# A transformer layer whose feed-forward products are taken seven at a time: the order of the seven, their PSUM banks, one held weight tile, and where W2's left factors are summed

## The chip, the cores and the metric

One core of a Trainium2 chip runs the whole layer in one program. The number given for a kernel is the device time of one execution, in microseconds (us).

## The reference, cut to what matters

The layer has 512 tokens of width 2048 and a feed-forward width of 8192, all in float32:

```python
mix = concat(rms_norm(windowed attention), rms_norm(dilated attention)) @ w_o
h   = layer_norm(ALPHA * x + mix)
ff  = square(relu(h @ w1)) @ w2                     # 2048 -> 8192 -> 2048
ple = (p @ w_ple) * sigmoid(h @ w_ple_gate)         # gate: 2048 -> 2048
out = layer_norm(ALPHA * h + ff + ple)
```

Only the gate, W1, W2 and the last norm are touched by the change. The attention part, up to 736.8 us, is the same text in both kernels.

## The kernel before, in words

**Seven products.** The gate, W1 and W2 are cut into 18 calls of `strassen`: two for the gate, eight for W1 (one for each chunk `n` of 1024 hidden columns), eight for W2 (`m` = 0 to 3 picks two chunks as the inner dimension, `c` = 0 or 1 the half of the output columns; the order is m0c0, m0c1, m1c0 and so on). A call multiplies a left matrix (tokens x inner) by a block of weights by Winograd's form of Strassen's method: each side is cut in four quarters, sums of quarters are the seven left factors s1 to s7 and the seven right factors, and the seven products p1 to p7 are added up into four quarters of the output. A product is summed over four slices `k` of the inner dimension, so a call has 28 steps (p, k) of 12 matmuls each: float32 is split into a high and a low part on either side, and three of the four part products are taken (`L598`, `L600`, `L601`).

**Right factors.** For each `k` the quarters b11, b12 and b22 are loaded (`wr` by SP's queue, `wk` by POOL's), and DVE makes b12 - b11 (`L610`) and b22 minus that (`L611`, kept in `wk`). In the second phase b21, b12 and b22 are loaded, b12 for the second time and b22 too, and DVE makes b22 - b12 (`L618`) and b21 - `wk` (`L619`). Every right factor is split by ACT (`wh`, `L579`) and DVE (`wl`, `L580`), with three buffers of each. `wr` has seven buffers and `wk` four.

**Left factors.** `factors` loads quarter blocks (`qh` of h for the gate and W1, `qf` of the squared hidden for W2, by ACT's queue at `L671`), forms s5, s6, s7 and s3 by DVE sums (`L547` to `L566`) and splits each factor by ACT (`L534`) and DVE (`L535`). For W2 this is done once for each `m`, with fourteen block loads and ten sums: the first half (s1, s5, s6) in the c = 1 call of the `m` before, the second half (s2, s7, s3, s4) in the first steps of the c = 0 call that uses them.

**PSUM and what reads it.** Three tiles a, b and c take the products: c holds p1 and then p2 on top of it, a holds p6, p7, p4 summed, b holds p5 and p3. In the gate and W1, `quarters` copies or adds what is complete into SBUF. In the gate the finished quarter is combined with `ple` and with `hk`, a block of h that TensorE transposes (`L693`). In W1 a finished quarter is transposed (`L707`), relu'd by ACT and squared by DVE (`L709`), and stored to `f_d`. In W2, ACT copies each product out (`ev`, `L793`) and POOL's queue adds it into DRAM (`z_d`, and `p1_d` for p1). For the last `m`, `last_sum` adds in SBUF instead: it loads `zl` from `z_d`, adds the products (`L740`), takes the norm's statistics, and `finish` writes two of the four token rows at a time.

**What sets the order.** `PHASES` fixes the order of the 28 steps; dictionaries of `between` steps (`mid`, `last`) hang the left factors' work in front of a step's number. All blocks that are not weights (`qh`, `qf`, `hk`, `pl`, the quarters `c`, `f`, `ev`, `zl`) share one pool of six 512 KB buffers, tag "o". A load that finds no free buffer waits on its queue, and what stands behind it in that queue waits with it.

Of the kernel before, what the change touches and what calls it, by code (L numbers as in the profile page):

```python
# [11 lines left out]
F32 = mybir.dt.float32  # L12
# [26 lines left out]
def block_kernel(ctx: ExitStack, tc: tile.TileContext, xT, pT, positions, w_in, w_o, w_gate, w_ple,  # L39
# [448 lines left out]
    for g in range(4):  # L488
        raw = raw_load(w_ple[g])
        wk = [split(raw[:, k * S:(k + 1) * S], "w", "w") for k in range(2)]  # L490
        for t in range(NQ):
# [6 lines left out]
            nc.scalar.dma_start(ple_d[t, g], e)  # L498
# [20 lines left out]
    opc = tc.tile_pool(name="op", bufs=1)  # L519
    op = opc.__enter__()  # L520
    ps = ctx.enter_context(tc.tile_pool(name="ps2", bufs=1, space=bass.MemoryType.PSUM))

    def o_tile(name, shape=(P, 2, S)):
        return op.tile(list(shape), F32, name=name, tag="o", bufs=OB)

    def factors(load, sg):


        q = {}

        def put(p, src):
            hi = sp.tile([P, 4, HS], R32, name=f"s{p}h", tag=f"s{p}h", bufs=2)
            lo = sp.tile([P, 4, HS], R32, name=f"s{p}l", tag=f"s{p}l", bufs=2)
            nc.scalar.activation(hi, src, AF.Copy)  # L534
            nc.vector.tensor_tensor(lo, src, hi.bitcast(F32), op=ALU.subtract)  # L535
            sg[p] = hi, lo

        def get(*ks):
            for k in ks:
                q[k] = load(k)  # L540

        def a1():
# [40 lines left out]
    def strassen(src, sg, read, between={}):  # L583


        bank = {c: ps.tile([P, 2, S], F32, name=c, tag=c, bufs=1) for c in "cab"}
        t2 = {}

        def prod(p, chain, k, w, first):
# [318 lines left out]
```

## Time and profile before

| what | value |
|---|---|
| median of 3 runs | 2374.33 us (2371.89 to 2377.45) |
| the profiled execution | 2366.62 us |
| its span, first to last instruction | 2364.8 us |
| mean granted TensorE clock over the span | 0.965 |
| busy, share of the span: TensorE, DVE, ACT, POOL | 92%, 71%, 43%, 5% |
| attention, up to the first `strassen` call | 736.8 us |
| gate, two calls | 209.4 us |
| W1, eight calls | 663.7 us |
| W2, eight calls | 729.2 us |
| after the last matmul | 25.6 us |

The stages begin and end where the matmuls of the 18 calls begin in the trace. Shares over the whole span hide that the stages differ: the stretches in the rows below, one for each call, are the unit to read. The granted clock is the throttle's: 1.00 is 2.4 GHz, and 0.5 of it is 1.2 GHz.

### The profile page before, as it was taken

The page shows a single profiled execution, that of the slowest core. Times are in us where ns is not written, and L with a number is a line of the kernel's source. Part 1 is how long each engine was busy: PE and PEld are TensorE (multiplying, and loading weights), DVE is VectorE, ACT ScalarE, POOL GpSimd, SP SyncE. Part 2 cuts the span into 40 slices and gives each one's busy share as a digit, 9 for nine tenths or more (in the row PEclk, how much of TensorE's full clock was granted, in tenths as well). Part 3 has the DMA queues.
Part 4 walks back from the last instruction along what each step waited for, and adds up shares of the span by engine and source line. Part 5 has one row for each costly group of instructions (what it writes and reads, how often), then busy time and mean ns, then how long its engine had stood idle before and what let it go on. Part 6 is the DMA issues. An engine that isn't in the chain of part 4 may idle for free. (4 is left out here: it accounts for less than half of the span.)

```text
span 2364.8 us, 26043 instructions
## 1 busy us (share of the span) xinstructions
PE 2171.0 (92%) x9672; PEld 1771.6 (75%) x9672; DVE 1683.8 (71%) x2035; ACT 1015.2 (43%) x1320; POOL 116.7 (5%) x152
## 2 busy tenths in 40 slices
PE   8999999999994988999999999997988988988895
PEld 7888888888873766887888888785766766766674
DVE  7676655555766866777777777779668568667888
ACT  5454443443335433444444444445445445444331
POOL 0000000000020000000000000000101101101000
PEclk9999999999997988999999999998999999988998
DMA  6222222233328656556555545556867867877682
GB/s 224 72 70 74 72 81 81 80 112 134 98 94 315 202 192 225 170 172 206 165 173 186 197 159 179 195 181 234 217 216 229 216 204 237 218 207 233 204 279 77
DMA packets 134943, 406.84 MB, mean 172 GB/s; under 512 B 13184, under 2 KB 24448, under 8 KB 134816
## 3 DMA queue, kind: packets, MB, share of 16 engines
q1 hardware_dynamic: 84512, 270.83, 34.2%
q0 software_dynamic: 22944, 64.08, 11.0%
q10 hardware_dynamic: 27360, 70.26, 8.2%
q8 instruction: 76, 1.25, 0.2%
q14 instruction: 51, 0.42, 0.1%
HBM read 347.45 MB, written 57.67 MB: 171 GB/s over the span
## 5 line engine op out<-in xcount | busy, mean ns | idle before, releaser
L579 ACT ACTIVATE wh<-wr 128x1024 fp32r<-128x1024 f32 x360 | 380.8, 1061 | 553.6 <-PE a L600 232.5
L580 DVE TENSOR_TENSOR wl<-wr,wh 128x1024 fp32r<-128x1024 f32 x360 | 434.9, 1220 | 50.3 <-ACT wh L579 49.6
L65 DVE TENSOR_TENSOR wl<-raw,wh 128x512 fp32r<-128x512 f32 x216 | 149.1, 691 | 163.9 <-ACT wh L64 131.5
L64 ACT ACTIVATE wh<-raw 128x512 fp32r<-128x512 f32 x216 | 135.7, 629 | 283.6 <-PE u L72 271.3
L71 PE MATMUL u<-xh,wh 128*128 128x512 f32 x576 | 227.4, 395 | 6.0 <-ACT xh L64 6.0
L72 PE MATMUL u<-xl,wh 128*128 128x512 f32 x576 | 225.4, 391 | 0.0
L73 PE MATMUL u<-xh,wl 128*128 128x512 f32 x576 | 225.3, 391 | 0.0
L579 ACT ACTIVATE wh<-wk 128x1024 fp32r<-128x1024 f32 x144 | 152.4, 1060 | 167.2 <-PE a L600 73.6
L580 DVE TENSOR_TENSOR wl<-wk,wh 128x1024 fp32r<-128x1024 f32 x144 | 174.6, 1218 | 19.3 <-ACT wh L579 19.3
L618 DVE TENSOR_TENSOR wr<-wr 128x1024 f32<-128x1024 f32 x72 | 88.1, 1223 | 116.2 <-DMA wr<-in_w 108.8
L598 PE MATMUL c<-wh,s1h 128*128 128x512 f32 x288 | 116.7, 405 | 34.3 <-DVE s5l L535 24.9
L610 DVE TENSOR_TENSOR wr<-wr 128x1024 f32<-128x1024 f32 x72 | 87.8, 1222 | 77.9 <-DMA wr<-in_w 73.3
L601 PE MATMUL b<-wl,s3h 128*128 128x512 f32 x288 | 116.2, 403 | 19.2 <-DVE wl L580 19.2
L601 PE MATMUL c<-wl,s1h 128*128 128x512 f32 x288 | 116.5, 404 | 17.7 <-DVE wl L580 17.7
L71 PEld LDWEIGHTS u<-xh,wh 128*128 128x128 f32 x576 | 108.6, 189 | 27.2 <-ACT xh L64 6.0
L611 DVE TENSOR_TENSOR wk<-wk,wr 128x1024 f32<-128x1024 f32 x72 | 87.9, 1220 | 56.6 <-DMA wk<-in_w 45.0
L601 PE MATMUL b<-wl,s5h 128*128 128x512 f32 x288 | 115.0, 399 | 14.0 <-DVE wl L580 14.0
L73 PEld LDWEIGHTS u<-xh,wl 128*128 128x128 f32 x576 | 108.5, 188 | 22.6
L598 PE MATMUL a<-wh,s6h 128*128 128x512 f32 x288 | 114.7, 398 | 11.5 <-ACT wh L579 11.5
L72 PEld LDWEIGHTS u<-xl,wh 128*128 128x128 f32 x576 | 108.6, 189 | 21.9 <-DVE xl L65 0.4
L601 PE MATMUL a<-wl,s6h 128*128 128x512 f32 x288 | 115.4, 401 | 8.9 <-DVE wl L580 8.9
L598 PE MATMUL a<-wh,s7h 128*128 128x512 f32 x288 | 114.0, 396 | 8.7 <-ACT wh L579 8.7
(240 smaller groups left out, 4881.5 us busy)
## 6 DMA issues: line engine op xcount, KB each, us to landing
wr<-in_w SPq DMA_DIRECT2D x320, 512.0 KB, 4.3
raw<-in_w_in SPq DMA_DIRECT2D x64, 512.0 KB, 3.7
wk<-in_w POOLq DMA_DIRECT2D x64, 512.0 KB, 5.0
qf<-f_d ACTq DMA_DIRECT2D x56, 512.0 KB, 5.4
wr<-in_w_gate SPq DMA_DIRECT2D x40, 512.0 KB, 4.7
z_d<-ev POOLq DMA_DIRECT2D x36, 512.0 KB, 8.5
raw<-in_w_o SPq DMA_DIRECT2D x32, 512.0 KB, 3.5
f_d<-f ACTq DMA_DIRECT2D x32, 512.0 KB, 3.5
```

Of the source, the lines that this page charges most:

```text
L64: nc.scalar.activation(hi, src, AF.Copy)
L65: nc.vector.tensor_tensor(lo, src, hi.bitcast(F32), op=ALU.subtract)
L71: nc.tensor.matmul(o, wh, ah, start=start, stop=False)
L72: nc.tensor.matmul(o, wh, al, start=False, stop=False)
L73: nc.tensor.matmul(o, wl, ah, start=False, stop=stop)
L579: nc.scalar.activation(hi, t, AF.Copy)
L580: nc.vector.tensor_tensor(lo, t, hi.bitcast(F32), op=ALU.subtract)
L598: nc.tensor.matmul(o, sh[:, i, x], w[0][:, c], start=first and k == 0 and j == 0, stop=False, skip_group_check=skip)
L601: nc.tensor.matmul(o, sh[:, i, x], w[1][:, c], start=False, stop=k == 3 and j == 1, skip_group_check=skip)
L610: nc.vector.tensor_tensor(t1, t1, b11, op=ALU.subtract)
L611: nc.vector.tensor_tensor(t2[k], t2[k], t1, op=ALU.subtract)
L618: nc.vector.tensor_tensor(t3, b22, t3, op=ALU.subtract)
```

## The change

`PHASES` becomes the flat table `STEPS`, with p3 and p7 in the middle and p2 and p4 last. Tile a now takes p1, p6, p7 and p4 as one running sum, b takes p5 and p3, and c takes p2 alone; a product on a is read between its last step and the next product's first step on a. `READ` says to which quarter each product goes; p1 is added into z's (0, 0) quarter, and `p1_d` is gone.

In W2 (`hold=True`) b12 is loaded once into tag "g" and kept for its second use, so a `k` costs five loads and not six. In W1 and the gate it is loaded twice, through tag "q".

After each W1 chunk the sums of W2's left factors are formed from the four squared quarters, and all seven factors are stored in `s_d` (three stores by ACT's queue, four by POOL's). The square moves from DVE to ACT. W2 then loads fourteen finished factors for each `m` by SP's queue (`qs`, two buffers) and only splits them: twelve in the c = 1 call before, two (`LATE`: s4 and s2 of the second chunk) in the c = 0 call.

The buffers are given out anew: `r` 4 (was `wr` 7), `q` 2, `k` 4, `g` 4, `c` 3, where there were six "o". `z_d` and `ple_d` have two token rows side by side, so that a partition's piece in DRAM is 4 KB and not 2 KB. `last_sum` does seven additions where there were ten, loads `zl` by SP and stores by POOL. `finish` runs for rows 2 and 3 after p4 and for rows 0 and 1 after p2.

```diff
-WB = {"wr": 7, "wk": 4, "wh": 3, "wl": 3}
-OB = 6
+WB = {"r": 4, "q": 2, "k": 4, "wh": 3, "wl": 3, "c": 3, "g": 4}
-    (((1, 0), (1, 1), (5, 0), (6, 0), (1, 2), (5, 1), (6, 1), (1, 3), (5, 2), (6, 2), (6, 3), (5, 3)), 1),
...
+STEPS = ((1, 0), (1, 1), (5, 0), (1, 2), (5, 1), (1, 3), (5, 2), (6, 0), (5, 3), (6, 1), (6, 2), (6, 3),
+         (3, 0), (7, 0), (3, 1), (7, 1), (3, 2), (7, 2), (3, 3), (7, 3),
+         (2, 0), (4, 0), (4, 1), (2, 1), (4, 2), (4, 3), (2, 2), (2, 3))
+LATE = {2: (12, 16), 4: (14, 18)}
-CHAIN = {1: ("c", True), 2: ("c", False), 6: ("a", True), 7: ("a", False), 4: ("a", False), 5: ("b", True),
+CHAIN = {1: ("a", True), 6: ("a", False), 7: ("a", False), 4: ("a", False), 5: ("b", True), 3: ("b", False),
+         2: ("c", True)}
+READ = {1: (0, 0), 2: (0, 0), 6: (0, 1), 3: (0, 1), 5: (1, 1), 7: (1, 1), 4: (1, 0)}
+LAST = (2, 3, 7, 4)
...
+    def f_factors(m, sg):
+        at = {False: {}, True: {}}
+        for p in range(1, 8):
+            for g in range(2):
+                def step(p=p, g=g):
+                    x = block("qs", "q")
+                    nc.sync.dma_start(x, s_d[2 * m + g, p - 1])
+                    put(sg[g], p, x)
+                late = p in LATE
+                at[late].setdefault(LATE[p][g] if late else STEPS.index((p, 2 * g + 1)) + 2, []).append(step)
+        return at
...
+        def factor(p, k):
+            if p == 1:
+                b11[k] = w_load(src(k, 0), "r")
+                b12[k] = w_load(src(k, 1), "g" if hold else "q")
+                t2[k] = w_load(src(k, 3), "k")
+                return b11[k]
+            if p == 5:
+                nc.vector.tensor_tensor(b11[k], b12[k], b11[k], op=ALU.subtract)
+                nc.vector.tensor_tensor(t2[k], t2[k], b11[k], op=ALU.subtract)
+                return b11[k]
...
+            if p == 3:
+                b22[k] = w_load(src(k, 3), "r")
+                if not hold:
+                    b12[k] = w_load(src(k, 1), "q")
+                nc.vector.tensor_tensor(b12[k], b22[k], b12[k], op=ALU.subtract)
+                return b22[k]
...
+            nc.vector.tensor_tensor(t2[k], b21[k], t2[k], op=ALU.subtract)
+            return t2[k]
...
-            nc.vector.tensor_tensor(f, f, f, op=ALU.mult)
-            nc.scalar.dma_start(f_d[n, 2 * th + nh], f)
+            nc.scalar.activation(y, y, AF.Square)
...
+                nc.vector.tensor_tensor(f[1, 1], f[1, 0], f[1, 1], op=ALU.add)
+                keep(5, f[1, 1])
+            if (th, nh) == (0, 0):
+                nc.vector.tensor_tensor(f[1, 0], f[0, 0], f[1, 0], op=ALU.subtract)
+                keep(7, f[1, 0])
+                nc.vector.tensor_tensor(f[1, 1], f[1, 1], f[0, 0], op=ALU.subtract)
+                keep(6, f[1, 1])
+                nc.vector.tensor_tensor(f[0, 1], f[0, 1], f[1, 1], op=ALU.subtract)
+                keep(3, f[0, 1])
```

**DVE at the start of a c = 0 call of W2 (m = 1), before.** `s2l`, `s7l` and the like are low parts of left factors, `qf<-qf` their sums, `wl` and `wr`, `wk` the right factors' low parts and sums:

```order
L580 TENSOR_TENSOR wl<-wr,wh 128x1024
L610 TENSOR_TENSOR wr<-wr 128x1024
L580 TENSOR_TENSOR wl<-wr,wh 128x1024
L611 TENSOR_TENSOR wk<-wk,wr 128x1024
L535 TENSOR_TENSOR s2l<-qf,s2h 128x1024
L560 TENSOR_TENSOR qf<-qf 128x1024
L580 TENSOR_TENSOR wl<-wk,wh 128x1024
L535 TENSOR_TENSOR s7l<-qf,s7h 128x1024
L565 TENSOR_TENSOR qf<-qf 128x1024
L535 TENSOR_TENSOR s4l<-qf,s4h 128x1024
L566 TENSOR_TENSOR qf<-qf 128x1024
L580 TENSOR_TENSOR wl<-wr,wh 128x1024 x2
```

Six of these twelve rows are left factors' work, between the splits that the call's own steps need. The same place after, where `qs` is a loaded factor and `wg` the held b12:

```order
L616 TENSOR_TENSOR wr<-wg,wr 128x1024
L533 TENSOR_TENSOR s4l<-qs,s4h 128x1024
L599 TENSOR_TENSOR wl<-wr,wh 128x1024
L617 TENSOR_TENSOR wk<-wk,wr 128x1024
L599 TENSOR_TENSOR wl<-wr,wh 128x1024
L616 TENSOR_TENSOR wr<-wg,wr 128x1024
L533 TENSOR_TENSOR s2l<-qs,s2h 128x1024
L599 TENSOR_TENSOR wl<-wr,wh 128x1024
L617 TENSOR_TENSOR wk<-wk,wr 128x1024
L599 TENSOR_TENSOR wl<-wr,wh 128x1024
L616 TENSOR_TENSOR wr<-wg,wr 128x1024
L599 TENSOR_TENSOR wl<-wr,wh 128x1024
```

Two rows of left factors' work are left, `s4l` and `s2l`; all sums are gone from here.

**ACT in the middle of a c = 1 call of W2 (m = 1), before,** from the tenth of the 28 splits on:

```order
L579 ACTIVATE wh<-wk 128x1024 x2
L793 ACTIVATE ev<-c 128x1024
L579 ACTIVATE wh<-wr 128x1024 x3
L793 ACTIVATE ev<-a 128x1024
L579 ACTIVATE wh<-wr 128x1024
L793 ACTIVATE ev<-b 128x1024
L671 DMA qf<-f_d 128x1024 x3
L534 ACTIVATE s1h<-qf 128x1024
L579 ACTIVATE wh<-wr 128x1024 x3
L534 ACTIVATE s5h<-qf 128x1024
L671 DMA qf<-f_d 128x1024 x2
```

The loads `qf` stand in ACT's own queue, and the split `s1h`, which waits for one of them, stands ahead of the weights' splits. After, where `ev<-a` at first is p1's copy and the second time p6's:

```order
L532 ACTIVATE s5h<-qs 128x1024
L598 ACTIVATE wh<-wr 128x1024
L792 ACTIVATE ev<-a 128x1024
L532 ACTIVATE s1h<-qs 128x1024
L598 ACTIVATE wh<-wk 128x1024 x3
L792 ACTIVATE ev<-b 128x1024
L532 ACTIVATE s5h<-qs 128x1024
L598 ACTIVATE wh<-wr 128x1024
L532 ACTIVATE s6h<-qs 128x1024
L598 ACTIVATE wh<-wg 128x1024
L598 ACTIVATE wh<-wr 128x1024
L792 ACTIVATE ev<-a 128x1024
```

The loads are no longer on ACT; a copy `ev<-a` stands one split behind the step that ended its product, and the splits of left factors stand singly between those of the weights.

**DVE in the second half of a W1 chunk, before** (`c` with a number is a quarter in SBUF, `f` the squared block):

```order
L580 TENSOR_TENSOR wl<-wr,wh 128x1024 x2
L610 TENSOR_TENSOR wr<-wr 128x1024
L580 TENSOR_TENSOR wl<-wr,wh 128x1024 x2
L610 TENSOR_TENSOR wr<-wr 128x1024
L580 TENSOR_TENSOR wl<-wr,wh 128x1024
L653 TENSOR_TENSOR c_9508<-c_9508,a 128x1024
L580 TENSOR_TENSOR wl<-wr,wh 128x1024
L709 TENSOR_TENSOR f<-f 128x1024
L610 TENSOR_TENSOR wr<-wr 128x1024
L580 TENSOR_TENSOR wl<-wk,wh 128x1024 x2
L709 TENSOR_TENSOR f<-f 128x1024
L653 TENSOR_TENSOR c_9490<-c_9490,b 128x1024
```

The squares are DVE's, and the second `wk` sums (`L619`) lie far ahead. The same half after, where p3's addition is the first of the two rows of `L671`:

```order
L599 TENSOR_TENSOR wl<-wq,wh 128x1024
L634 TENSOR_TENSOR wk<-wr,wk 128x1024
L599 TENSOR_TENSOR wl<-wr,wh 128x1024
L599 TENSOR_TENSOR wl<-wq,wh 128x1024
L634 TENSOR_TENSOR wk<-wr,wk 128x1024
L599 TENSOR_TENSOR wl<-wr,wh 128x1024
L671 TENSOR_TENSOR c_9525<-c_9525,b 128x1024
L599 TENSOR_TENSOR wl<-wk,wh 128x1024
L671 TENSOR_TENSOR c_9475<-c_9475,a 128x1024
L599 TENSOR_TENSOR wl<-wk,wh 128x1024
L599 TENSOR_TENSOR wl<-wr,wh 128x1024
L599 TENSOR_TENSOR wl<-wk,wh 128x1024 x2
```

The last of four sums `L634`, each of which needs a b21 load of its own, now stands in front of the additions that the transposes wait for; the square is not on DVE.

## Rows read from the trace of the kernel before

**Rows 1.** Page, part 2: granted clock and DMA in 40 equal slices.
```profile
PEclk9999999999997988999999999998999999988998
DMA  6222222233328656556555545556867867877682
```

**Rows 2.** Stretches: span and length; PE, PEld, DVE, ACT, POOL (instructions); clock; DMA share; GB/s.
```profile
736.80:851.70 114.90, 90.77 (x369) 70.97 (x369) 94.77 (x86) 49.50 (x49) 2.11 (x4) 0.89 0.70 238
851.70:946.20 94.50, 86.32 (x370) 70.38 (x369) 65.39 (x61) 35.17 (x34) 2.11 (x4) 0.92 0.59 199
1110.50:1192.30 81.80, 80.26 (x369) 66.16 (x369) 61.95 (x53) 35.69 (x39) 2.11 (x4) 1.00 0.55 180
1519.80:1609.90 90.10, 81.50 (x378) 66.83 (x376) 66.16 (x57) 38.59 (x43) 2.11 (x4) 0.99 0.57 195
1609.90:1703.10 93.20, 82.16 (x336) 64.17 (x337) 74.31 (x65) 46.68 (x47) 9.09 (x10) 0.94 0.73 217
1703.10:1790.00 86.90, 78.89 (x338) 64.13 (x337) 62.83 (x54) 41.72 (x42) 10.28 (x11) 0.94 0.76 222
1790.00:1884.60 94.60, 83.03 (x337) 64.10 (x336) 67.13 (x59) 43.61 (x44) 10.74 (x11) 0.96 0.77 220
1884.60:1973.40 88.80, 79.79 (x337) 64.31 (x336) 62.71 (x54) 41.71 (x42) 10.72 (x11) 0.94 0.77 217
...
2157.00:2261.00 104.00, 84.43 (x337) 66.49 (x336) 81.41 (x74) 38.14 (x38) 3.39 (x5) 0.89 0.67 222
2261.00:2339.20 78.20, 76.89 (x337) 62.73 (x335) 65.68 (x74) 27.61 (x26) 0.00 (x0) 1.00 0.47 166
2339.20:2364.80 25.60, 0.02 (x1) 0.00 (x0) 21.58 (x62) 0.00 (x0) 0.00 (x0) 0.60 0.43 164
```

**Rows 3.** DMA issues, 1790 to 2157 us: transfers, KB each, median us to landing.
```profile
wr<-in_w SPq DMA_DIRECT2D x81, 512.0 KB, 4.7
qf<-f_d ACTq DMA_DIRECT2D x28, 512.0 KB, 6.4
z_d<-ev POOLq DMA_DIRECT2D x24, 512.0 KB, 8.1
```

**Rows 4.** Timeline, 1914 to 1918 us: start, duration, instruction, [idle before it].
```profile
1914.88 1.06 ACT L579 ACTIVATE wh<-wr 128x1024 fp32r<-128x1024 f32 x1 [1.66 <-PE a L600]
1914.91 0.39 PE L598 MATMUL b<-wh,s5h 128*128 128x512 f32 x1
...
1915.85 1.00 ACT L793 ACTIVATE ev<-a 128x1024 f32<-128x1024 f32 x1
...
1917.63 0.39 PE L598 MATMUL c<-wh,s2h 128*128 128x512 f32 x1
```

**Rows 5.** Stretch inside the call that starts at 1790.0 us, columns as in group 2.
```profile
1805.00:1812.00 7.00, 5.28 (x15) 3.35 (x14) 7.00 (x7) 5.14 (x6) 0.00 (x0) 0.76 0.91 304
```

**Rows 6.** ACT timeline, 1917 to 1936 us.
```profile
1917.89 0.81 ACTq L671 DMA_DIRECT2D qf<-f_d  x2
...
1924.35 1.06 ACT L534 ACTIVATE s1h<-qf 128x1024 fp32r<-128x1024 f32 x1 [4.78 <-DMA qf<-f_d]
```

**Rows 7.** DVE timeline of the same stretch.
```profile
1928.47 1.23 DVE L618 TENSOR_TENSOR wr<-wr 128x1024 f32<-128x1024 f32 x1 [8.39 <-DMA wr<-in_w]
```

**Rows 8.** Waits of TensorE, 736.8 to 2339 us: us in total, times, longest.
```profile
PE pt L693 <- DMA hk<-h_d: 16.2, 5, 4.8
PE pt L707 <- DVE c L653: 13.7, 9, 1.8
```

**Rows 9.** DMA issues, 1110.5 to 1519.8 us, five W1 chunks, columns as in group 3.
```profile
wr<-in_w SPq DMA_DIRECT2D x100, 512.0 KB, 3.9
```

**Rows 10.** DVE timeline at the program's end.
```profile
2332.58 0.25 DVE L764 BATCH_NORM_AGGREGATE mv<-bs 128x2 f32<-128x24 f32 x1
...
2359.54 1.41 DVE L775 SCALAR_TENSOR_TENSOR zl<-zl,r,gb 128x512 f32<-128x512 f32 x2
```

**Rows 11.** TensorE timeline at the program's end.
```profile
2338.83 0.39 PE L601 MATMUL a<-wl,s4h 128*128 128x512 f32 x1
```

More of the change, by code (lines that the diff above doesn't have):

```diff
@@ L497, in block_kernel @@
             nc.scalar.activation(e, o, AF.Copy)
-            nc.scalar.dma_start(ple_d[t, g], e)
+            nc.scalar.dma_start(ple_d[t // 2, g, :, t % 2], e)
     for j in range(NT):
@@ L560, in b2 @@
             nc.vector.tensor_tensor(q[2], q[0], q[2], op=ALU.subtract)
-            put(7, q[2])
+            put(sg, 7, q[2])
         def b3():
@@ L581, in w_split, with strassen @@
         return hi, lo
[L583 to L589, printed above, removed]
+    def strassen(src, sg, read, hold=False, between={}):
+        bank = {c: ps.tile([P, 2, S], F32, name=c, tag=c, bufs=1) for c in "abc"}
+        b11, b12, b21, b22, t2 = {}, {}, {}, {}, {}
+        def factor(p, k):
[8 more added lines that the diff above has]
+                return b11[k]
+            if p == 6:
+                return t2[k]
[5 more added lines that the diff above has]
+                return b22[k]
+            if p == 7:
+                return b12[k]
+            if p == 2:
+                b21[k] = w_load(src(k, 2), "r")
+                return b21[k]
+            if k not in b21:
+                b21[k] = w_load(src(k, 2), "r")
+            nc.vector.tensor_tensor(t2[k], b21[k], t2[k], op=ALU.subtract)
+            return t2[k]
+        for n, (p, k) in enumerate(STEPS):
+            for f in between.get(n, ()):
+                f()
+            chain, first = CHAIN[p]
+            if p == 2 and k in b21:
+                wh, wl = w_split(b21[k])
+            else:
+                wh, wl = w_split(factor(p, k))
             sh, sl = sg[k // 2][p]
@@ L597, in prod @@
                     o = bank[chain][:, t]
[L598 removed]
+                    nc.tensor.matmul(o, sh[:, i, x], wh[:, c], start=first and k == 0 and j == 0, stop=False,
                                      skip_group_check=skip)
[L600 to L601 removed]
+                    nc.tensor.matmul(o, sl[:, i, x], wh[:, c], start=False, stop=False, skip_group_check=skip)
+                    nc.tensor.matmul(o, sh[:, i, x], wl[:, c], start=False, stop=k == 3 and j == 1,
                                      skip_group_check=skip)
@@ L694, in gated, with squared @@
                 nc.vector.scalar_tensor_tensor(g[:, i], pt, ALPHA, g[:, i], op0=ALU.mult, op1=ALU.add)
-            nc.scalar.dma_start(z_d[2 * th:2 * th + 2, n].rearrange("t p s -> p t s"), g)
-        strassen(lambda k, q, c=c: w_gate[c, q, k], sh, quarters(gated), mid if c == 0 else {})
+            nc.scalar.dma_start(z_d[th, n], g)
+        strassen(lambda k, q, c=c: w_gate[c, q, k], sh, quarters(gated), between=mid if c == 0 else {})
     sf = [{}, {}]
-    early, late = zip(*(factors(load_f(g), sf[g]) for g in range(2)))
+    at = f_factors(0, sf)
     for n in range(NFC):
-        def squared(th, nh, x, n=n):
-            f = o_tile("f", (P, 4, HS))
+        f = {}
+        def squared(th, nh, x, n=n, f=f):
+            f[th, nh] = y = block("f")
             for i in range(2):
```

208 lines of the change are left out of this document (70 added, 138 removed), and 2 rows, old and new, of the table PHASES.

## The prediction

> **What bounds the kernel now.** I read the page's 40 slices first. The granted clock and the DMA's share change character about a third of the way in [rows 1]: from there the 18 seven-product calls run, with the DMA at five to eight tenths and dips of the clock to 7 to 9 tenths. So I cut the trace at the first matmul of every call [rows 2].
>
> A call's floor comes from a timeline. The first matmul of one step starts at 1914.91 and the first of the next at 1917.63 [rows 4]: 2.72 us for a step of 12 matmuls, so 28 steps cost 76.2 us. The W1 chunks take 81.8 us at a clock of 1.00, and 32 transposes are in that: TensorE bounds them, but for a short wait of up to 1.8 us for DVE's last addition at the transposes [rows 8]. The very last W2 call, with nothing added into DRAM and no factors to prepare, takes 78.2 us with DVE busy 65.7. The other W2 calls take 86.9 to 104.0: six of them, from 1703.1 to 2261.0, 557.9 us against a floor of 6 x 76.2 = 457.2. These 100.7 us are where the time lies, and two places explain most of them.
>
> In the c = 0 calls DVE is the bound for a time: in the 7 us from 1805 it is busy 7.00 while TensorE gets 15 matmuls done and the clock falls to 0.76 [rows 5]. What it does beside the call's own work are 14 instructions of left factors (8 splits, 6 sums), all near the start. In the c = 1 calls DMA is: three `qf` loads go out from 1917.89, ACT's split of the first starts at 1924.35 after 4.78 us of idleness [rows 6], and DVE waits 8.39 us for a weight that arrives behind them [rows 7].
>
> **The change part by part.**
>
> *DVE's work in W2.* A DVE instruction of this size costs 62.71/54 = 1.16 us [rows 2]. The ten sums for each `m` go (11.6 us of DVE), and the c = 0 call keeps 2 left-factor instructions where it had 14: 13.9 us leave the stretch in which DVE was the bound. What DVE has left there is 28 splits, 16 sums and 2 left factors, 46 x 1.16 = 53 us in 76.2. TensorE is then the bound and the nearest row is the last call's 78.2; I take 79.5, since seven additions into DRAM stay. The c = 1 call has 28 + 16 + 12 = 56, 65 us, as much as the last call's 65.7 within 78.2.
>
> *DMA in W2.* Per `m` there were 48 weights, 14 blocks and 14 additions, 76 transfers of 512 KB; from 1790.0 to 1973.4 the share was 0.77 of 183.4 us, 1.86 us of all 16 engines for each. Held b12 makes it 68. By call: c = 0 has 20 weights + 2 + 7 = 29, 54 us in 79.5 (0.68); c = 1 has 20 + 12 + 7 = 39, 73 us, which in 80 us would be 0.91. No call of before held more than 0.77, so the c = 1 call will not be free of waits, above all where eight weights, several factors and three additions fall in the steps of p3 and p7. I take 83 (78.2 if it hides, 88.8 as before if it does not). Calls 1703.1, 1884.6 and 2066.3 at 83, the two middle c = 0 calls at 79.5, and the last c = 0 call at 80: 488 instead of 557.9, **-70**. The call at 2157.0, the slowest with 104.0, loses most: its ten additions of products become seven and its loads leave ACT's queue. The last call, 78.2 before, I put at +1.
>
> *The factor loads' queue.* They move from ACT's queue to SP's, with two buffers. A factor load that waits for its buffer now holds up the weight loads behind it, but ACT no longer issues, and the splits stand singly between those of the weights. A weight takes 4.7 us to land here, a block 6.4 [rows 3].
>
> The Trainium skill (DMA: Bandwidth & Descriptors, Issuing engines are not separate DMA queues) states that transfers from SP, ACT and GpSimd run on the same 16 engines and interleave, so a change of queue alone brings no bandwidth. The trace agrees as far as it goes: weights on SP waited 8.39 us behind blocks on ACT [rows 6, 7]. By that rule W2's gain would be only what the eight transfers and the DVE work bring; it is the ground of the second rival.
>
> *Bank a shared by p1, p6, p7 and p4.* The copy must lie between the end of a product and the next product's first step on a, one step of 2.72 us. Before, the same sequence on ACT without this bound: p6 ended at 1914.91, ACT did a split until 1915.94 and the copy `ev<-a` until 1916.85, 1.94 us after the end [rows 4]. That leaves 0.8 us. I take nothing; fully exposed it would be about 2 us at each of three borders in 18 calls, 108 us. The Trainium skill (PSUM — Partial Sum Buffer, Summary: rules for kernel authors) advises to read a bank other than the one matmuls write; here the reader and the writer take turns on a. By the row the turn fits in a step; by the rule's plain reading it would be the 108 us, which I keep as a rival.
>
> *W1.* A chunk gets three more stores; on DVE four sums come, four squares go to ACT and two additions become copies: 53 instructions [rows 2] become 51. New is a chain: b21 of a slice takes the buffer that b22 of the same slice leaves, and `L634` needs it. Split and sum 2 x 1.16, landing 3.9 [rows 9], 0.2 to start: 6.4 us for a slice, where two steps last 5.44. Over the four slices DVE loses 4 us of the lead that three split buffers give it (about 5), and p3's addition and so the transposes behind it come 1 us later than now: the wait of 1.5 to 1.8 us [rows 8] becomes 2 to 3. I take +0.3 for each of seven chunks, and nothing for the last (90.1 before [rows 2]), which hands its factor work from ACT to SP but fetches ten factors between its weights: together **+2**, with -10 if the lead holds and +25 if the stall reaches 3 us and the clock falls with it.
>
> *W1 to W2.* The first W2 call (93.2 before) must fetch its held b12 into buffers that the last chunk's squared blocks leave. Behind the last W1 step stand an addition and a sum (2.3), transposes, relu and square (2 to 3) and a store, which I estimate at the 3.9 of a load [rows 9]: about 9 us. Then come the load (4.7), a subtraction and a split (2.3): 16 us, of which the two steps of p1 that need no b12 cover 5.4. TensorE will stand for about 10 us and the clock fall for some 4 more; with 3 us of the usual waits that is the 17.0 us over the floor that this call had before, when left factors made DVE busy 74.3. I take **+1**, between -10 and +10.
>
> *Gate.* 209.4 us before. The transposes waited 16.2 us for `hk` [rows 8], whose buffer came from the shared pool of six; now it has four of its own kind. DVE was busy 94.8 of 114.9 in the first call and still has some 90, so that can't go below about 95. I take 105 and 84: **-20** (-5 to -30).
>
> *End.* Before, the first `finish` began at 2332.58, 6.5 us ahead of the last matmul's end (2338.83 + 0.23 [rows 10, 11]), and DVE worked through to 2360.95. After, `finish` comes after p4, two steps of splitting later, so some 3 us ahead: more of the same DVE work lies behind the last matmul. **+2.5**.
>
> **Sum.** -70 + 1 + 2 + 1 - 20 + 2.5 = -83.5 against the profiled execution of 2366.6, hence 2283. That execution lies 7.7 us under the median of the runs shown; on the median's scale the forecast is 2374.3 - 83.5 = 2290.8, and I give 2289, a little toward the profile's own scale.
>
> **The rivals.**
>
> *All of W2 at TensorE's pace.* The DMA crowd in c = 1 dissolves since the additions now move 4 KB pieces: six calls at 78.2 make 469, 19 less than above; the gate gains its 30, W1 its 10. For it: the last call's 78.2. Against: 0.91 of the DMA's time. 2289 - 19 - 10 - 12 = 2248. Chance 0.15.
>
> *Starved weights.* Four `r` buffers where seven stood, behind factor loads in one queue: the c = 1 calls stay at 88.8 and the c = 0 calls fall to 85 only, W1 pays its 25. For it: weights already land 4.7 us after issue and DVE waited 8.39. Against: fewer transfers, and b12 held. 2289 + 3 x 5.8 + 3 x 5.3 + 23 = 2345. Chance 0.17.
>
> *Slower: the turn on bank a is exposed.* If the split ahead of the copy on ACT is itself late, which happens from the point where ACT runs over 0.8 us behind the step, TensorE waits about 2 us at each of 54 borders: 2289 + 108 = 2397, and more if the clock follows. For it: a factor's split now stands ahead of the copy in c = 1. Against: the row's 0.8 us, and ACT is busy half the time. Chance 0.06.
>
> *No effect:* the gain in W2 is eaten by W1 and the hand-over, about 2374. Chance 0.02.
>
> **How the numbers follow.** The forecast has 0.60. Its own range is 2265 to 2315: W2's six calls 470 to 505, the gate's ±10, W1's. For eight in ten I reach into both neighbours, 2243 to 2343. A difference under 0.2% (4.7 us) can't be told from none. Faster takes the forecast and the first two rivals, 0.92; same 0.02; slower 0.06.
>
> **What would show it.** Right: W2 calls of c = 0 near 79 to 80 and of c = 1 near 83, with no DVE wait of 8 us for a weight; a gate under 195; the call after W1 with its 10 us stall at the first subtraction of b12; copies from a that end within a step. Wrong: TensorE idle just ahead of p6's, p7's or p4's first matmul (bank a); W1 chunks over 84 with waits at `L634`; DVE's waits for weights in c = 1 as long as before; a gate over 200.

## The result, and the profile after

The changed kernel takes 2264.7 us (2262.9 to 2266.7, 4 runs) where the kernel before, in the same runs, takes 2373.1: a ratio of 0.9549, with a 95% interval of 0.9517 to 0.9581. The forecast was 2289 with a range of 2243 to 2343, so the kernel is 24 us faster than forecast and within the range. The profiled execution has a span of 2261.1 us, 103.7 less than before, and a mean granted clock of 0.982 (0.965 before).

The stretches of the changed kernel, one for each call of which the prediction speaks (columns as in [rows 2], to which they answer):

```profile
740.20:838.70 98.50, 89.30 (x361) 69.28 (x362) 87.15 (x79) 50.22 (x50) 2.12 (x4) 0.92 0.76 264
838.70:919.60 80.90, 80.89 (x374) 66.31 (x372) 65.03 (x61) 37.95 (x37) 2.11 (x4) 1.00 0.65 228
1080.40:1161.20 80.80, 80.33 (x370) 66.12 (x369) 60.04 (x52) 41.48 (x45) 4.25 (x8) 1.00 0.57 202
1486.10:1576.60 90.50, 83.86 (x369) 66.80 (x368) 70.39 (x61) 50.74 (x56) 4.25 (x8) 0.98 0.70 244
1576.60:1669.40 92.80, 82.44 (x346) 66.30 (x345) 62.05 (x54) 40.17 (x41) 9.58 (x14) 0.94 0.70 207
1669.40:1751.00 81.60, 78.03 (x337) 62.47 (x336) 62.84 (x55) 46.05 (x46) 8.30 (x11) 1.00 0.82 240
1751.00:1830.90 79.90, 77.56 (x337) 62.60 (x336) 55.47 (x48) 38.85 (x38) 8.26 (x11) 1.00 0.72 202
1830.90:1911.60 80.70, 78.01 (x337) 62.52 (x337) 62.92 (x55) 45.95 (x46) 8.25 (x11) 1.00 0.82 243
2072.20:2155.90 83.70, 79.14 (x338) 63.75 (x337) 65.71 (x60) 33.14 (x33) 4.64 (x8) 0.98 0.62 206
2155.90:2232.50 76.60, 76.41 (x337) 62.79 (x335) 63.81 (x65) 27.51 (x26) 2.64 (x5) 1.00 0.35 124
2232.50:2261.10 28.60, 0.18 (x1) 0.00 (x0) 24.40 (x72) 0.00 (x0) 0.00 (x0) 0.58 0.38 147
```

Read downwards: the gate's second call and a middle W1 chunk (1080.40) run at a clock of 1.00 in 81 us, the last chunk (1486.10), which fetches W2's first factors, takes 90.5, the hand-over from W1 to W2 (1576.60) is as bad as it was, and the middle calls of W2 are 80 to 82 us at 1.00, with a DMA share of 0.82 in c = 1 (1669.40, 1830.90) and 0.72 in c = 0 (1751.00). By stage, from the spans (the last matmul ends at 2232.7, 0.2 us into the last row):

| stage | before | after | difference | forecast |
|---|---|---|---|---|
| gate, from 736.8 us | 209.4 | 182.8 | -26.6 | -20 |
| W1, eight chunks | 663.7 | 657.0 | -6.7 | +2 |
| first W2 call | 93.2 | 92.8 | -0.4 | +1 |
| six W2 calls behind it | 557.9 | 486.5 | -71.4 | -70 |
| last W2 call | 78.2 | 76.8 | -1.4 | +1 |
| behind the last matmul | 25.6 | 28.4 | +2.8 | +2.5 |

The copy out of bank a, on ACT and on TensorE (answering to [rows 4]):

```profile
1848.14 1.06 ACT L598 ACTIVATE wh<-wr 128x1024 fp32r<-128x1024 f32 x1 [0.76 <-PE a L655]
1849.10 1.01 ACT L792 ACTIVATE ev<-a 128x1024 f32<-128x1024 f32 x1
```

```profile
1848.12 0.39 PE L653 MATMUL b<-wh,s5h 128*128 128x512 f32 x1
...
1851.07 0.39 PE L653 MATMUL a<-wh,s6h 128*128 128x512 f32 x1
```

p1 ends at 1848.12, the copy at 1850.11, and p6's first matmul on a comes at 1851.07, directly behind the matmul ahead of it: 0.96 us to spare. From 1669 to 2156 us TensorE has no listed wait for a copy `ev`.

The hand-over: what SP's queue waits for from 1576 to 1597 us, its issue of the held b12 (`wg`), and DVE's first subtraction of it:

```profile
SPq L592 <- DMA s_d<-f: 11.0, 4, 4.4
```

```profile
1587.16 8.49 SPq L592 DMA_DIRECT2D wg<-in_w  x4
```

```profile
1591.64 1.22 DVE L616 TENSOR_TENSOR wr<-wg,wr 128x1024 f32<-128x1024 f32 x1 [3.62 <-DMA wg<-in_w]
```

Each of the four loads of b12 waits for a store of the last chunk's blocks to land and leave its buffer; the first can go out 10 us after the call began, and DVE has it 4.5 us later.

TensorE's waits for transposes, 736.8 to 2233 us (answering to [rows 8]; `L694` is the gate's, `L710` W1's), and a W1 chunk's last b21 sum and p3's addition on DVE:

```profile
PE pt L710 <- DVE c L671: 7.2, 8, 2.1
...
PE pt L694 <- issue: 0.5, 1, 0.5
```

```profile
1132.13 1.22 DVE L634 TENSOR_TENSOR wk<-wr,wk 128x1024 f32<-128x1024 f32 x1 [1.97 <-DMA wr<-in_w]
...
1134.41 1.21 DVE L671 TENSOR_TENSOR c<-c,b 128x1024 f32<-128x1024 f32 x1
```

The wait for `hk` is gone (16.2 us before), that for W1's additions halved (13.7 before), although `L634` waits 1.97 us for its load ahead of the addition.

DMA issues in W2, 1751 to 2072 us (answering to [rows 3]), and DVE's last work (answering to [rows 10]):

```profile
wr<-in_w SPq DMA_DIRECT2D x48, 512.0 KB, 4.7
z_d<-ev POOLq DMA_DIRECT2D x28, 512.0 KB, 6.6
qs<-s_d SPq DMA_DIRECT2D x26, 512.0 KB, 5.1
```

```profile
2229.74 0.38 DVE L767 BATCH_NORM_AGGREGATE mv<-bs 128x2 f32<-128x24 f32 x2
...
2255.71 1.41 DVE L778 SCALAR_TENSOR_TENSOR zl<-zl,r,gb 128x512 f32<-128x512 f32 x2
```

A weight lands as late as before (4.7 us), a factor sooner (5.1, before 6.4). The longest wait of DVE for a weight, from 1669 to 2156 us, is 5.3 us, where it was 8.4. The first `finish` starts 2.8 us ahead of the last matmul's end, where it was 6.5.

### The profile page after: what moved, and what is told of

Same layout as the page of the kernel before. It is cut to its first block, busy times and chain, and to the rows that moved or that the text cites. A ratio compares the mean times of both kernels' runs of the same rounds, so it can differ in the third digit from the quotient of the medians.

```text
span 2261.1 us, 26072 instructions
## 1 busy us (share of the span) xinstructions
PE 2144.7 (95%) x9672; PEld 1757.3 (78%) x9672; DVE 1612.5 (71%) x1969; ACT 1061.6 (47%) x1372; POOL 124.3 (5%) x192
## 4 chain that ended last, share of the span: by engine, by line
PE 76%; DMA 9%; DVE 9%; issue 3%; ACT 2%; DVEq 0%; SPq 0%; ACTq 0%
PE u L72 9%; PE u L71 9%; PE a L656 9%; PE u L73 9%; PE a L653 9%; PE a L655 8%; DMA wr<-in_w 5%; PE b L656 4%; PE b L653 4%; PE b L655 4%; DVE wl L599 4%; PE c L656 2%; PE c L653 2%; PE c L655 2%; DMA qs<-s_d 2%
## 5 line engine op out<-in xcount | busy, mean ns | idle before, releaser
L598 ACT ACTIVATE wh<-wr 128x1024 fp32r<-128x1024 f32 x288 | 303.8, 1059 | 345.2 <-PE a L655 194.0
L599 DVE TENSOR_TENSOR wl<-wr,wh 128x1024 fp32r<-128x1024 f32 x288 | 350.2, 1221 | 96.5 <-ACT wh L598 93.3
L598 ACT ACTIVATE wh<-wk 128x1024 fp32r<-128x1024 f32 x144 | 152.6, 1060 | 179.3 <-PE b L655 89.5
L634 DVE TENSOR_TENSOR wk<-wr,wk 128x1024 f32<-128x1024 f32 x72 | 88.2, 1224 | 97.1 <-DMA wr<-in_w 91.2
L653 PE MATMUL a<-wh,s1h 128*128 128x512 f32 x288 | 114.8, 399 | 30.7 <-DMA qh<-h_d 29.3
L653 PE MATMUL b<-wh,s5h 128*128 128x512 f32 x288 | 116.6, 405 | 12.1 <-ACT wh L598 12.1
L656 PE MATMUL c<-wl,s2h 128*128 128x512 f32 x288 | 113.3, 393 | 6.0 <-DVE wl L599 5.7
L656 PE MATMUL a<-wl,s1h 128*128 128x512 f32 x288 | 114.8, 399 | 2.4 <-DVE wl L599 2.4
L655 PE MATMUL b<-wh,s5l 128*128 128x512 f32 x288 | 115.5, 401 | 0.0
L656 PE MATMUL a<-wl,s7h 128*128 128x512 f32 x288 | 113.0, 392 | 1.2 <-DVE wl L599 1.1
```

The costliest lines, as they stand in the source:

```text
L598: nc.scalar.activation(hi, t, AF.Copy)
L599: nc.vector.tensor_tensor(lo, t, hi.bitcast(F32), op=ALU.subtract)
L634: nc.vector.tensor_tensor(t2[k], b21[k], t2[k], op=ALU.subtract)
L653: nc.tensor.matmul(o, sh[:, i, x], wh[:, c], start=first and k == 0 and j == 0, stop=False, skip_group_check=skip)
L655: nc.tensor.matmul(o, sl[:, i, x], wh[:, c], start=False, stop=False, skip_group_check=skip)
L656: nc.tensor.matmul(o, sh[:, i, x], wl[:, c], start=False, stop=k == 3 and j == 1, skip_group_check=skip)
```

## The experiments

Above each result stands what was expected before the run. The ratios are to the kernel before in the same session; differences in us are to the changed kernel's 2264.7, measured in another session, and a few us of them are noise. Spans of single calls come from one profiled execution each. This table has the W2 calls of c = 0 for m = 1 and 2 and those of c = 1 for m = 0, 1 and 2, first matmul to first matmul:

| kernel | c = 0 (two calls) | c = 1 (three calls) | ratio to before |
|---|---|---|---|
| before | 94.6, 92.9 | 86.9, 88.8, 90.7 | 1 |
| changed | 79.9, 80.9 | 81.7, 80.7, 79.6 | 0.9549 |
| b12 loaded twice | 81.9, 79.1 | 85.2, 84.8, 86.1 | 0.9664 |
| factors on ACT's queue | 79.2, 80.1 | 91.4, 85.5, 80.8 | 0.9648 |
| DVE work given back | 83.6, 83.5 | 82.4, 80.0, 79.3 | 0.9586 |
| 2 KB rows | 80.7, 79.8 | 78.3, 79.1, 79.5 | 0.9542 |
| eight late factors | 78.6, 77.6 | 85.6, 81.8, 79.0 | 0.9521 |
| the same, DVE work | 82.0, 78.7 | 84.0, 84.6, 79.2 | 0.9596 |
| the same, chain, ACT's queue | 85.4, 83.0 | 86.9, 83.1, 85.5 | 0.9645 |
| the same, b12 twice | 94.6, 94.0 | 87.1, 87.3, 83.6 | 0.9714 |

**b12 loaded twice.**

```diff
-            strassen(..., read if more else last_sum(c), True, mid)
+            strassen(..., read if more else last_sum(c), False, mid)
```

> The changed kernel, with b12 loaded twice again in W2 (through the two q buffers) instead of held. My theory: W2's gain has several causes and the held tile is a small one. Eight transfers for each m come back, some 15 us of the DMA's time; the c = 1 calls (80.7 now) grow by 2 to 4 us, the c = 0 calls by 0 to 1, while the first W2 call, which now waits 7 us for the held b12 behind the last chunk's blocks, gets 6 to 9 shorter: the whole is 0 to +8 us. Rival: the held tile is what made W2 faster; the calls grow by 6 us and more each, the whole by over 35.

Measured: 2291.4 us, 27 more than the changed kernel. The c = 1 calls grow by 4.7 on average, c = 0 not at all, and the first W2 call falls from 92.7 to 80.8. The part not foreseen lies in the last two calls, 101.2 and 82.0 where they were 83.7 and 76.8: there, by the kernel's text, `zl` takes one of the two q buffers and the weights have one left. The held tile is worth some 5 us in a c = 1 call and costs 12 in the first call; the rival's 35 for it falls, and so does "0 to +8" for the whole.

**The factors' loads on ACT's queue.**

```diff
-                    nc.sync.dma_start(x, s_d[2 * m + g, p - 1])
+                    nc.scalar.dma_start(x, s_d[2 * m + g, p - 1])
```

> The changed kernel, with the fourteen factor loads for each m on ACT's queue again. My theory: a load that waits for one of its two buffers holds up ACT's splits; the c = 1 calls grow by 3 to 5 us each and show TensorE waiting for splits, the c = 0 calls (2 loads) by under 1: +10 to +18 in all. Rival: the queue does not matter, since the transfers are the same: within 4 us.

Measured: 2286.8 us, +22. The three c = 1 calls grow by 15.7 together and the last chunk, which loads ten factors, by 3.8; c = 0 stays. The queue matters more than forecast, with the same bytes. Where it costs time, in the first c = 1 call (ACT, then TensorE):

```profile
1756.70 1.06 ACT L532 ACTIVATE s4h<-qs 128x1024 fp32r<-128x1024 f32 x1 [8.63 <-DMA qs<-s_d]
```

```profile
1758.76 0.50 PE L653 MATMUL c<-wh,s2h 128*128 128x512 f32 x1 [3.40 <-ACT wh L598]
```

ACT stands 8.63 us in front of a factor's split, for the factor's load; a weight's split stands behind it, and TensorE waits for that.

**DVE work given back.** The sums go to a PSUM tile that nothing reads in W2.

```diff
+            if n in extra:          # steps 1 to 12 of c = 0, m = 1, 2, 3
+                for i in range(2):
+                    pt = ps.tile([P, S], F32, name="pt", tag="pt", bufs=2)
+                    x = slice(i * S, (i + 1) * S)
+                    nc.vector.tensor_tensor(pt, wh.bitcast(F32)[:, x], wl.bitcast(F32)[:, x], op=ALU.add)
```

> The changed kernel, with DVE work given back: in steps 1 to 12 of the c = 0 calls of m = 1, 2, 3, two more 128x512 additions into an unused PSUM tile for each step, in all as long as the 12 instructions that the change took away there; no transfer is added. My theory: that work was the bound in the first half of the c = 0 calls; they grow by 8 to 14 us each, DVE stands back to back there and the clock dips: +25 to +40. Rival: the c = 0 calls were slow for their loads, so without these the work hides: under +6.

Two stretches of a c = 0 call of this kernel (columns as in [rows 2]):

```profile
1763.00:1775.00 12.00, 9.44 (x39) 6.64 (x38) 12.00 (x14) 3.83 (x5) 0.00 (x0) 1.00 0.15 56
1775.00:1787.00 12.00, 12.00 (x52) 9.61 (x53) 12.00 (x16) 5.95 (x6) 1.71 (x2) 1.00 0.53 132
```

DVE is busy for the whole of both stretches, just as in [rows 5], and for 69.5 us of this call (m = 1), more than the 67.1 of before. TensorE has 39 matmuls in the first stretch and its full 52 in the second: the c = 0 calls of m = 1, 2, 3 grow by 3.7, 2.6 and 1.1 us only, the whole by 9. My reason for the c = 0 calls falls: a full DVE is not enough. What differs is the DMA: its share is 0.15 and 0.53 here, and 0.91 in [rows 5]. So DVE's work together with a crowd of loads is not excluded by this run.

**2 KB rows.** `z_d` gets its old shape `[NQ, 4, P, S]`, with the rearranged views that go with it.

> The changed kernel, with z laid out in DRAM as before, 2 KB for each partition and row and not 4 KB. My theory: an addition into DRAM lands a microsecond later, nobody waits for it, 0 to +5 us. Rival: the longer pieces are what let the c = 1 calls run at 80.7 where 83 was forecast; then these calls grow by 3 us and more and the whole by 10 to 20.

Measured: 2262.3 us, no difference; the additions land in 7.5 us (7.2 with 4 KB, 1675 to 2072 us). The layout is worth nothing here.

**Eight late factors.**

```diff
-LATE = {2: (12, 16), 4: (14, 18)}
+LATE = {2: (1, 5), 7: (2, 6), 3: (3, 7), 4: (4, 8)}
```

> The changed kernel, with the table LATE set so that eight of the fourteen factors (s2, s7, s3, s4 of both chunks) are loaded and split from the first steps of the c = 0 call on, as before the change, and six in the c = 1 call. Giving back DVE work alone cost only some 3 us for a c = 0 call, so half of my theory fell. New theory: the c = 0 calls before were slow by two things together, a crowd of loads at their start that takes DVE's lead away, and then DVE work that keeps it from coming back. Then the crowd alone costs 2 to 5 us for each of the calls of m = 1, 2, 3 with c = 0 (79.9, 80.9, 83.7 now), and the c = 1 calls get 1 to 3 us shorter. Rival: the loads' place alone made the 94.6 and 92.9 of before; then the c = 0 calls grow by over 9 us each.

Measured: 2256.1 us, a ratio of 0.9521 with an interval of 0.948 to 0.9562, which overlaps the changed kernel's. The c = 0 calls get shorter (78.6, 77.6, and 79.7 for m = 3), not longer, and two of the three c = 1 calls longer, not shorter. But the run doesn't do what it was made for. The factor loads in the c = 0 call of m = 1, in the kernel before and in this one:

```profile
qf<-f_d ACTq DMA_DIRECT2D x8, 512.0 KB, 5.2
```

```profile
qs<-s_d SPq DMA_DIRECT2D x4, 512.0 KB, 4.8
```

The table LATE names eight, but in the trace only two of these four loads are late factors, the other two being the next m's first; the rest of the eight go out in the c = 1 call before. The call of m = 2 is the same. For m = 3 six late factors are loaded in the call, spread over 35 us, and it takes 79.7 where it took 83.7. So late loads that are spread out cost nothing by themselves; the crowd of before, eight within 18 us, was not tested.

**The same with DVE work** (one 128x512 addition for each of steps 1 to 12).

> The kernel with eight late factors, and twelve 128x512 DVE additions in steps 1 to 12 of the c = 0 calls of m = 1, 2, 3 in the place of the six sums: with them such a call has the loads, the splits and about the DVE instructions of before (58). New theory (crowd and DVE work together): c = 0 calls of 86 to 94 us, more than the sum of what either costs alone. Rival: the two add up only, 83 to 86; what is missing to 94 is then in the old order of the products or in the sums that splits on ACT waited for.

Measured: 2273.9 us; 82.0 and 78.7, and 88.9 for m = 3. For m = 1 and 2, with at most four factor loads in the call, the two about add up, as the rival said. For m = 3, with five, the additions cost 9.2 us (79.7 to 88.9), though twice as many cost 1.1 in the changed kernel: more than the sum, as the theory said. So the run speaks for neither side alone.

**The same with the chain, on ACT's queue** (without the additions).

```diff
-                    nc.sync.dma_start(x, s_d[2 * m + g, p - 1])
+                    nc.scalar.dma_start(x, s_d[2 * m + g, p - 1])
+                    for _ in range({5: 1, 6: 1, 7: 1, 3: 2}.get(p, 0)):
+                        nc.vector.tensor_tensor(x, x, x, op=ALU.max)
                     put(sg[g], p, x)
```

> The kernel with eight late factors, and with the way of the left factors as it was before: their loads on ACT's queue, and five DVE instructions for each chunk (x = max(x, x), which leaves the values) between a loaded block and its split on ACT, where the sums stood. DVE, ACT and the queue have what they had, but for the step order, the banks and the held b12. My theory now: what made the c = 0 calls slow was the chain from a load over a DVE sum to ACT's split, in the same two queues that the weights need, and not the number of DVE instructions: c = 0 calls of 85 to 92 us for m = 1, 2, 3 (78.6, 77.6, 79.7 without the chain), c = 1 calls of 82 to 88. Rival: under 82 for c = 0; then the old order of the steps, with its sixth load for each slice, carries the rest of W2's gain.

Measured: 2289.0 us. The c = 0 calls take 85.4, 83.0 and, for m = 3, 83.1: one of three in the range expected, all above the rival's 82. The c = 1 calls are in their range. Again the c = 0 calls of m = 1 and 2 issue four factor loads, two of them late factors.

**And b12 loaded twice for m = 0, 1, 2.**

> The same kernel as the one with the chain, and b12 loaded twice in W2 for m = 0, 1, 2. Of the change in W2 only the step order, the banks, 4 KB rows and the number of buffers are left. If the left factors' way and the sixth load are all, the calls of m = 1 and 2 with c = 0 take 90 to 95 us and those with c = 1 87 to 92, as before the change. Rival: if the order of the steps and the shared bank carry over a third of the gain, the c = 0 calls stay under 86.

Measured: 2305.2 us. The c = 0 calls are where the theory had them, and of the c = 1 calls (87.1, 87.3, 83.6) all but the last.

The c = 0 call of m = 1, in the four kernels with eight late factors, with chain, and with chain and double load, and in the one with the double load alone:

```profile
1753.10:1831.70 78.60, 77.06 (x338) 62.82 (x337) 57.43 (x50) 39.33 (x39) 8.28 (x11) 1.00 0.75 209
```

```profile
1759.80:1845.20 85.40, 78.47 (x337) 62.45 (x336) 64.32 (x56) 39.72 (x39) 8.28 (x11) 1.00 0.71 202
```

```profile
1756.30:1850.90 94.60, 80.66 (x337) 63.70 (x336) 66.94 (x58) 42.73 (x42) 8.25 (x11) 0.95 0.73 211
```

```profile
1741.10:1823.10 82.00, 79.05 (x338) 63.83 (x337) 56.62 (x49) 39.55 (x39) 8.27 (x11) 0.98 0.77 225
```

ACT's queue and the chain together cost 5 to 7 us (78.6 to 85.4, 77.6 to 83.0); no run has eight late factors on this queue without the stand-ins, so the two are not told apart. The sixth load alone costs little (82.0, 79.1, where the changed kernel has 79.9, 80.9), and all together 16 (94.6, 94.0): the two calls are as long as before the change, with DVE busy for 67 us of them, as in [rows 2], and the clock at 0.95. Other than in the two kernels above, the call now does hold most of the factors' work:

```profile
qs<-s_d ACTq DMA_DIRECT2D x7, 512.0 KB, 5.1
```

Six of the seven are late factors, where the kernel with b12 held has two: the last step is not the sixth load alone. How it looks from inside the last kernel (ACT, then DVE; `L586` is the stand-in for a sum, `L600` the weights' split), and what TensorE waits for from 1756 to 1795 us:

```profile
1779.61 3.43 ACTq L584 DMA_DIRECT2D qs<-s_d  x2
1788.86 1.06 ACT L532 ACTIVATE s7h<-qs 128x1024 fp32r<-128x1024 f32 x1 [8.68 <-DVE qs L586]
1789.82 1.04 ACT L600 ACTIVATE wh<-wr 128x1024 fp32r<-128x1024 f32 x1
```

```profile
1787.60 1.23 DVE L586 TENSOR_TENSOR qs<-qs 128x1024 f32<-128x1024 f32 x1 [4.91 <-DMA qs<-s_d]
```

```profile
PE b L655 <- ACT wh L600: 6.8, 1, 6.8
```

ACT stands 8.68 us in front of a factor's split, which waits for DVE's stand-in, which waits 4.91 for the factor's load; the splits of three weights stand behind it, and TensorE waits 6.8 us for them. In [rows 6], in a c = 1 call, it is the same form: 4.78 us in front of a split while weights wait. In the c = 0 call of m = 3 of the kernel before, the slowest with 104.0, it is larger (ACT's loads, ACT, TensorE):

```profile
2158.79 14.78 ACTq L671 DMA_DIRECT2D qf<-f_d  x3
```

```profile
2173.61 1.06 ACT L534 ACTIVATE s2h<-qf 128x1024 fp32r<-128x1024 f32 x1 [14.72 <-DMA qf<-f_d]
```

```profile
2175.67 0.80 PE L598 MATMUL a<-wh,s6h 128*128 128x512 f32 x1 [8.93 <-ACT wh L579]
```

The third of the three loads goes out only at the end of the first row, and ACT stands until then; TensorE's longest wait in this call is 2.9 us after the change. No run puts this call back (79.7 to 88.9 in the kernels with eight late factors).

For the c = 0 calls of m = 1 and 2 the form is not the same. TensorE's longest waits in the call at 1790.0 of the kernel before:

```profile
PE a L601 <- DVE wl L580: 5.0, 3, 1.8
PE b L601 <- DVE wl L580: 4.1, 4, 1.6
```

They are short waits for DVE's low parts, none over 1.8 us, and hardly any for ACT; in the last kernel half of the waiting is the one wait of 6.8 us for ACT. Two calls of equal length that wait for different things do not show one cause. A second reserve: with b12 in q, the weights share two buffers with the factors, which they didn't before the change, so the size of the last step may be partly that.

**Three copies out of bank a** for p1, p6 and p7.

```diff
-                nc.scalar.activation(e, b, AF.Copy)
+                for _ in range(3 if p in (1, 6, 7) else 1):
+                    nc.scalar.activation(e, b, AF.Copy)
```

> The changed kernel, with ACT's copy of p1, p6 and p7 out of bank a in W2 (m = 0, 1, 2) done three times over, 2 us more for each. My theory: a copy ends 0.8 to 1.0 us before the next product on a begins, so 1.0 to 1.2 us of the added 2 are exposed at each of 18 borders: +15 to +28 us with what the clock may add, and TensorE idle just ahead of the first matmul of p6, p7 and p4. Rival: the turn on bank a has more room than the rows show, or ACT's other work moves around it: under +6. Other rival: the copies were already exposed, then +36 and more.

Measured: 2280.6 us, +15.9, or 0.9 us for each of 18 borders; the five calls behind the first grow by 15.0. ACT and TensorE around one of the borders:

```profile
1856.99 1.01 ACT L793 ACTIVATE ev<-a 128x1024 f32<-128x1024 f32 x1
...
1860.69 1.03 ACT L793 ACTIVATE ev<-a 128x1024 f32<-128x1024 f32 x1
```

```profile
1861.10 0.50 PE L656 MATMUL b<-wl,s5h 128*128 128x512 f32 x1 [1.53 <-DVE wl L599]
```

The size is as expected, the place is not: TensorE waits in the step between, for a weight's low part (1.53 us), since the copies push the next splits back on ACT. Its waits from 1669 to 2156 us, in this kernel, and the first of them in the changed kernel:

```profile
PE b L656 <- DVE wl L599: 15.0, 14, 2.5
PE c L653 <- ACT wh L598: 6.6, 5, 1.6
...
PE a L653 <- ACT ev L793: 0.9, 5, 0.2
```

```profile
PE b L656 <- DVE wl L599: 6.4, 9, 1.2
```

The waits in these first two lines grow by 15 us together (the second was 0.3 in the changed kernel), and those for a copy are 0.9 in all. In this run the turn on bank a is bounded by ACT's queue before it is by the bank.

**hk with buffers of its own, in the kernel before.**

```diff
-            hk = o_tile("hk", (P, 4, HS))
+            hk = wp.tile([P, 4, HS], F32, name="hk", tag="hk", bufs=2)
-WB = {"wr": 7, "wk": 4, "wh": 3, "wl": 3}
+WB = {"wr": 5, "wk": 4, "wh": 3, "wl": 3}
```

> The kernel before, with one thing changed: hk, the block of h that TensorE transposes in the gate, has two buffers of its own (taken from the seven of the weights, five left). My theory: the gate's gain (209.4 to 182.8 from 736.8 on, 10 more than forecast) is mostly that hk no longer waits in a shared pool: the two gate calls take 185 to 197 us together and TensorE's wait for hk is under 3 us. W1 and W2 may lose from the fewer weight buffers; only the gate is read here. Rival: the gate's gain comes from the new order and the copies moved to ACT; the gate stays above 202.

Measured: 2433.5 us in all, since five weight buffers slow the W1 chunks to 84 to 88 us (the last to 96.9). The gate's calls take 110.7 and 89.5 after a start that comes 7 us later, 207.2 counted as above: the expectation is missed, and the rival's "above 202" holds. But the second call was 12.7 us longer than a W1 chunk (94.5, 81.8) and is 3.6 longer here (89.5, 85.9 for the mean of five chunks), which puts some 9 us of its excess down to `hk`; that is argued from a kernel whose every call is slower, and not shown. For the first call the run decides nothing, and the gate's -26.6 is only in part explained.

**The square on DVE.**

```diff
-            nc.scalar.activation(y, y, AF.Square)
+            nc.vector.tensor_tensor(y, y, y, op=ALU.mult)
```

> The changed kernel, with the square of a W1 chunk's blocks on DVE again and not on ACT: 32 instructions, 4 for each chunk. W1's chunks take 80.8 us where they took 81.8 and 82 were forecast. Theory: the transposes' wait went with the new places of p3 and p7, which end 8 and 9 steps before the call does and whose additions find DVE ahead; DVE has slack and the chunks stay at 80.5 to 81.3, the whole within 4 us. Rival: the square on ACT is what freed DVE for those additions: the chunks go back to 81.8 or more, the whole grows by 7 and more.

Measured: 2271.3 us, +6.6, with intervals that overlap; the calls tell more: the seven chunks that carry no W2 factors take 577.6 us (566.4 changed, 573.6 before). The rival holds for the time, by one profile of each kernel: all of W1's gain is in moving the square, and without it W1 would have lost a little, as forecast. It doesn't hold for the place: in these seven chunks TensorE's waits at the transposes are 11.1 us before, 5.1 in the changed kernel and still only 6.2 here, as the theory said; what comes is 3.9 us of short waits for DVE's low parts, and the rest of the 11 us stands in no listed wait.

**A faster version.**

```diff
-            strassen(..., read if more else last_sum(c), True, mid)
+            strassen(..., read if more else last_sum(c), (m, c) != (0, 0), mid)
+LATE_LATER = {2: (1, 5), 7: (2, 6), 3: (3, 7), 4: (4, 8)}   # for m = 1, 2, 3
```

> A version that may beat both: the changed kernel, with the first W2 call not holding b12 (it loads it twice through q, as W1 does, and so waits for no block of the last W1 chunk), and with eight late factors for m = 1, 2, 3 (four for m = 0, as now). My theory: the first W2 call falls from 92.7 to about 81 and the last chunk to 88.5, the c = 0 calls to 78 to 79.5: 2241 to 2250 us, 15 to 23 under the changed kernel. Rival: the q buffers are crowded in the first call, or the c = 1 calls grow by what the c = 0 calls save: 2254 and more.

Measured: 2253.4 us (2250.3 to 2255.5), ratio 0.9493 with an interval of 0.9477 to 0.9509, below that of the changed kernel. The first W2 call falls to 84.1 and c = 0 to 78.3 and 77.5, but the last W1 chunk takes 91.7 and two c = 1 calls 84.8 and 84.4: 11 us where 15 to 23 were hoped for, nearly the rival's 2254. The six calls behind the first take 485.0 where they took 486.5, so the gain is in the first call, and against the kernel with eight late factors alone (2256.1, two runs) it is not clear of noise.

## Why the prediction was right, and where not

The time lay where the forecast put it, in the six W2 calls, and their sum (486.5 for 488) is right, in part by luck: the three c = 1 calls came 7 us under the 83 taken for each, and the three c = 0 calls 5.5 over. The 20 us by which the kernel gained more than the sum of -83.5 lie in W1 (8.7), the gate (6.6) and all of W2 (5.2). Of its steps:

*DVE's work in W2* was the wrong reason for a right number. DVE back to back [rows 5] was a sign, not the bound by itself: the same work, free of loads, costs 1 to 4 us a call where 12 to 15 went (94.6 to 79.9, 92.9 to 80.9). Before, TensorE did wait for DVE's low parts in these calls, with the DMA at 0.91 in the same row. What the runs show in its place is that the left factors' loads, sums and splits cost time by where they stand: in ACT's queue with the sums 5 to 7 us, and 16 when the sixth load and most of the factor loads are in the call too. Which of these carries how much stays open for m = 1 and 2, and so does the theory of a crowd of loads with DVE work behind it. For m = 3 the trace before has ACT standing 14.72 us in front of one split, and the prediction named that queue and had this call lose most; it lost 20.3.

*DMA in W2.* A share of 0.91 was forecast for the c = 1 calls and 0.82 measured; they took 80.7 and not 83; the price of a transfer was right as a mean over both calls (0.82 x 80.7 and 0.72 x 79.9 us for 68, 1.82 each, against 1.86) and wrong for either alone. With the same transfers, the queue alone is worth 22 us, by what stands behind a load that waits (8.63 us on ACT in that run). The Trainium skill (DMA: Bandwidth & Descriptors, Issuing engines are not separate DMA queues) says that issuing from several engines saves only the time that it takes to initiate a transfer; these 22 us come on top of that, and the measurement decides.

*Bank a* at nothing was right: 0.96 us to spare, where 0.8 was forecast, and 0.9 lost for each border when the copies take 2 us more. The Trainium skill (PSUM — Partial Sum Buffer, Summary: rules for kernel authors) advises to read another bank than the one matmuls write; taking turns cost no listed wait here, while ACT keeps its place.

*W1* failed at the square: its move to ACT was counted as two instructions fewer on DVE and priced at nothing beside the new chain. It is worth 11 us over seven chunks; the chain is there (`L634` waits 1.97 us) and reaches TensorE little.

*The hand-over* came as worked out in its order, with the stand at the first subtraction of b12; TensorE's wait there is 6.9 us, where about 10 were taken. *The gate* gained 6.6 more than I took, within the range; `hk` has not four buffers of its own, as the prediction says, but shares the four of tag g with `pl` and the blocks of h. *The end* lost 2.8 for 2.5. Two small readings: the 0.2 us "to start" in W1's chain stands in no row, and the last matmul's 0.23 us is 0.39 in [rows 11], which makes the 6.5 us 6.6; neither changes the sum.

## What to carry to other kernels

A full engine in a slow stretch shows where the work is, not what it waits for: put the work back alone, without its loads, before it is called the bound. A load that waits, in a queue that other work needs, costs more than its own time, since it holds what stands behind it; load what is finished, from a queue with little behind it. When a run is meant to move work from one call to another, count it in the trace first: a table in the source does not say where the instructions run. When a tile is held to save a load, look at whose buffers it needs at the first use.

## What the runs showed of the hardware

Fourteen factor loads for each m, issued by ACT and not by SP, cost 22 us with the same bytes. Twenty-four 128x512 additions more on DVE, busy then for 69.5 us of a call of 83.6, made calls of 80 to 84 us 1.1 to 3.7 us longer. Additions into DRAM by 4 KB or 2 KB pieces land in 7.2 and 7.5 us and cost the program the same.
